# A layer with a bidirectional state-space mixer: output weights summed by DMA, fills of the scan divided anew, groups and regions in natural order

## Chip, core and metric

The kernel runs on one core of one Trainium2 chip. The metric is device time in microseconds, from the run's start to its end. A profiled execution has a second, slightly shorter figure, its span from the first to the last instruction; all places in the trace are microseconds from the start of that span. The engines are named as in the profile: PE (TensorE, with PEld its weight load), DVE (VectorE), ACT (ScalarE), POOL (GpSimd), SP (SyncE, which here only issues DMAs). "ACTq" or "SPq" is an instruction that the engine's sequencer does itself, such as issuing a DMA.

## What is computed

One layer over 1024 latent tokens of 1024 channels, with 256 context tokens ahead of them. All numbers are float32. Cut to what matters here:

```python
h_l = modulate(rms_norm(x, norm_mix), m_l[0], m_l[1])    # m_l, m_c: six rows each of silu(c) @ ada_w + ada_b
h_c = modulate(rms_norm(ctx, norm_mix), m_c[0], m_c[1])
# S5: 64 groups of 16 channels, 64 complex states each, two directions; the latent scan starts from the context's last state
lam_bar = exp(lam * exp(log_step)); b_bar = ((lam_bar - 1) / lam)[..., None] * b
h[t] = lam_bar * h[t-1] + b_bar @ u[t];   y[t] = real(c @ h[t])
y = y_fwd + y_bwd + d_skip * h_l
g = gelu(y)
x = x + m_l[2] * (g * sigmoid(g @ w_glu + b_glu))
h = modulate(rms_norm(x, norm_ffn), m_l[3], m_l[4])
x = x + m_l[5] * ((silu(h @ w1) * (h @ w3)) @ w2)
out = rms_norm(x, norm_final)
```

## The kernel before

**Chunks and quarters.** The tokens are cut into chunks of T = 8: 32 chunks of context and 128 of latents, 160 columns. The 64 groups are handled in four quarters q of 16, and for the products in eight blocks of 8. A chunk's contribution to the state comes from products (`sums`, in the loop over `hb`), and lands in `STQ[q]`, a view of the large region `ra`: 160 columns, real and imaginary part, 16 entries (a group pair of one direction each). `ra` is 80.5 KB per partition, 20.125 KB for each quarter; the first 4 KB of each quarter's part hold the context's columns, which are dead once the context's last state (column 31) is known.

**The scan** (`scan`, L790) runs on DVE over all quarters at once: 32 steps that advance two chunks, on the odd columns of the first half, then 63 steps of one chunk. A step is four dependent instructions. The even columns of the first half are filled in behind it from their neighbours ("fills": `fill_ops`, four instructions for four columns of half a quarter, on DVE, one or two dropped into each step by `one`; `fill`, L818, on POOL, four instructions for 16 columns of half a quarter). Before, DVE fills quarters 0, 2 and 3, POOL quarter 1.

**What runs beside the scan** is a list written by hand, the string that `run` (L909) walks through. The order within each engine's queue, and on each engine that issues DMAs, is the order of that string; engines wait for each other by semaphores. Its letters:

- A n: the adaLN gate rows, up to weight tile n of 64 (`ada`, L510): one product per tile of 256 KB, which SP loads eight tiles ahead into stages in the regions c2 and c1 (`stg`). M0, M1, M2 (`mod_cols`, L825): the finished rows are copied by ACT into `r8`, turned by PE, copied again, and finished on POOL.
- L q: load quarter q's C matrices into `Cs[q % 2]` (L634), a DMA issued by ACT; G q: sign them on ACT (`cs_sign`, L637).
- C q p: piece p of quarter q's output weights (`cl_gen`, L643): two POOL products of 128x1024, one into the weights `CL[q]` (region c q), one into an operand buffer `ct`; then their sum. Quarter 0 sums on PE (two products with the identity per half, and ACT copies the sum back), quarters 1 to 3 by a DMA that accumulates, issued by POOL (L658).
- K (`k_mats`, L757): the kernel matrices of half a quarter, out through two small staging buffers to DRAM by ACT's queue (L773); T u (`toeplitz`, L775): read back by SP as a banded matrix for the block half u, into four places `KQ`, which lie in the context columns of quarters 2 and 3. B q: move quarter q's input matrices for K into the place of the powers that C 0 and C 1 have used up.
- R k, P k, Y (L936 to L943): for block k, ACT copies the early states (columns 31 to 94) into `HSe` in eight instructions, PE multiplies inputs and early states into two PSUM tiles (of three), ACT copies them to `Y`, which lies over the inputs.
- F: a fill on POOL. Z i: the first two copies of late states (`late_restack`, L904), shared by ACT, DVE and POOL.

**Behind the list** a loop (L1039) takes the eight blocks in the order `order`: late products (`late_mm`), their sum into `Y`, GELU, the turned halves (`gt_hi`, `gt_lo`) into regions that the output weights leave free, and the first GLU products. Then come the GLU and the SwiGLU network, which hold PE from about 305 us to the end.

**Regions.** c0 to c3 are 16 KB each: the output weights of quarter q, and before and after them stages, operands and the GLU's tiles. `rxc` (8 KB) has both `Cs` places, later two `HSl` places and weights; its second half is also the operand buffer of C32 and C33, since `Cs[0]` is dead by then.

Of the kernel before, what the change touches and what calls it, by code (L numbers as in the profile page):

```python
# [11 lines left out]
R32 = mybir.dt.float32r  # L12
# [5 lines left out]
P = 128  # L18
# [5 lines left out]
T = 8  # L24
G = 64
HC = 16
# [11 lines left out]
def s5_ffn_kernel(tc, a, out):  # L38
    nc = tc.nc
    V, S, E, PE, SY = nc.vector, nc.scalar, nc.gpsimd, nc.tensor, nc.sync  # L40
    ctx = ExitStack()
    with ctx:
        ctx.enter_context(tc.manual_schedule())
        sb = ctx.enter_context(tc.tile_pool(name="sb", bufs=1))
        def region(tag, kb, dt=F32):
            return sb.tile([P, int(kb * 256)], dt, tag=tag, name=tag)

        def view(reg, kb, shape, parts=P):
            off = int(round(kb * 256))
            n = int(np.prod(shape))  # L50
            v = reg[:parts, off:off + n]
            if len(shape) > 1:
                names = "abcdef"[:len(shape)]
                v = v.rearrange(f"p ({' '.join(names)}) -> p {' '.join(names)}",
                                **{k: d for k, d in zip(names, shape)})
            return v

        R0 = region("r0", 7)
        RA = region("ra", 80.5)
# [51 lines left out]
        STB = 20.125  # L111
# [476 lines left out]
        def rot(*args):  # L588
            for op in rot_ops(*args):
                op()  # L590
# [46 lines left out]
        def cs_sign(q):  # L637
            S.activation(Cs[q % 2][:, 0], Cs[q % 2][:, 0], AF.Copy, scale=sgn[:, 1:2])
            S.activation(Cs[q % 2][:, 1], Cs[q % 2][:, 1], AF.Copy, scale=-1.0)
# [3 lines left out]
        def cl_gen(q, part, ct, how):  # L643
# [15 lines left out]
            else:  # L659
# [10 lines left out]
                 7: [(1, [0], 0, 8)], 8: [(1, [0], 8, 16)], 9: [(1, [1, 2, 3])],  # L670
                 11: [(2, [0], 0, 8)], 12: [(2, [0], 8, 16)], 13: [(2, [1, 2, 3])],
                 14: [(3, range(4), 0, 8)]}
        ct0 = [view(RC[1], i, [8, T, HC]) for i in (12, 4)]
        ct1 = [view(RC[3], i, [8, T, HC]) for i in (0, 4)]
        for hb in range(16):
            sums(hb)
            ada1(1, *ADA1.get(hb, ()))
# [63 lines left out]
        st1, st2 = (t[:, 384:512].rearrange("p (q r e) -> p q r e", r=2, q=4) for t in (LTb, ltc))  # L741
        sf = [LTa[:, 384:448], LTa[:, 448:512]]
        cs_load(1, S)
        cs_sign(1)
        kt = pA.tile([P, 2, 240], F32, tag="r3", name="kt")
        S.copy(kt.rearrange("p a b -> p (a b)"), cpk[:, 0:1].to_broadcast([P, 480]))

# [37 lines left out]
        def fill_ops(q, h, j):  # L785
            st = STQ[q][:, :, :, 8 * h:8 * h + 8]
            o = rot_ops(st[:, 32 + 8 * j:39 + 8 * j:2], st[:, 31 + 8 * j:38 + 8 * j:2], LQ[0], 16 * q + 8 * h, V, sf)
            return [o[0], o[2], o[1], o[3]]

        def scan():  # L790
            rest = []

            def one():
                if rest:
                    rest.pop(0)()

            def step(lq, i, o):
                products(st1, st2, STE[:, i], lq)
                tt(STE[:, o], st1, STE[:, o], ADD)
                one()  # L800
                tt(STE[:, o], st2, STE[:, o], ADD)
                one()

            for k in range(32):
                step(LQ[1], 31 + 2 * k, 33 + 2 * k)
                if k % 4 == 3:
                    for d in range(2):
                        rest.extend(fill_ops(0, d, k // 4))
            for q in (2, 3):
                for j in range(8):  # L810
                    for d in range(2):
                        rest.extend(fill_ops(q, d, j))
            for k in range(64, 127):
                step(LQ[0], 31 + k, 32 + k)
            while rest:
                one()

        def fill(q, h, reg, kb):  # L818

            tmps = [view(reg, kb + i, [256]) for i in range(2)]  # L820
            st, c0 = STQ[q], 32 * h
            for e in (0, 8):
                rot(st[:, 32 + c0:63 + c0:2, :, e:e + 8], st[:, 31 + c0:62 + c0:2, :, e:e + 8], LS[:, 0], 16 * q + e, E, tmps)

        def mod_cols(part):  # L825
            r8 = view(RC[2], 0, [4, P])
            if part == 0:
                S.copy(r8, pm.rearrange("p (j n) -> p j n", j=4))
            elif part == 1:
                pt = pw()  # L830
                for j in range(4):
                    PE.transpose(pt[:, j], r8[:, j], ident)
                for h in range(2):
                    S.copy(mcol[:, :, 4 * h:4 * h + 4].rearrange("p b j -> p j b"), pt[:, :, h:P:32])
            elif part == 2:
                tt(mcol, mcol, modb[:, 2:6], ADD, E)
                E.tensor_copy(mod2[:, 0], mcol[:, 1])
                tt(mod2[:, 1], mcol[:, 2], epsc[:, 1:2].to_broadcast([P, T]), ADD, E)
                tt(mod2[:, 1], mod2[:, 1], nrm[:, 1], MUL, E)
# [8 lines left out]
        def hstate(reg, kb):  # L848

            return view(reg, kb, [2, 2, 2, 64, 2])  # L850
# [42 lines left out]

        scan()
        inner, hse = {}, {}
        ct2 = [view(RC[3], i, [8, T, HC]) for i in (8, 12)]
        ct3 = [view(RXc, 4, [8, T, HC])]
        cts = [ct0 * 2, ct1 * 2, ct1 * 2, ct2 + ct3 * 2]

        HSl = [hstate(RXc, 0), hstate(RXc, 4), hstate(RA, STB), hstate(RA, 2 * STB)]  # L900
        HSe = [hstate(*((RC[3], 8 + 4 * (i % 2)) if i < 4 else (RA, STB * (i % 2)))) for i in range(8)]
        order = (6, 7, 4, 5, 0, 1, 2, 3)

        def late_restack(i):  # L904

# [3 lines left out]
        def run(prog):  # L909


            for w in prog.split():
                op, i = w[0], int(w[1:])
                if op == "A":
                    ada(i)
                elif op == "M":
                    mod_cols(i)
                elif op == "K":
                    k_mats(*divmod(i, 2))
                elif op == "Z":  # L920
                    late_restack(i)
                elif op == "L":
                    cs_load(i, S)
                elif op == "G":
                    cs_sign(i)
                elif op == "B":
                    j = 48 - HC * i
                    S.copy(BBc[:, :, :, j:j + HC], BB[:, :, HC * i:HC * i + HC].rearrange("p d g h -> p g d h"))
                elif op == "C":
                    q, part = divmod(i, 10)  # L930
                    cl_gen(q, part, cts[q][part], HOW[q][part])
                elif op == "F":
                    fill(*divmod(i, 10), *((RC[3], 4) if i < 20 else (RXc, 4)))
                elif op == "T":
                    toeplitz(i)
                elif op == "R":  # L936
                    hse[i] = HSe[i]
                    for d in range(2):
                        restack(hse[i], 4 * i, d, 0, (S, S, S, S))
                elif op == "P":  # L940
                    inner_mm(i, hse[i])
                elif op == "Y":
                    S.copy(yview(i), inner[i])  # L943

        HOW = ((PE,) * 4,) + ((SY,) * 4,) * 3
        run("A8 A12 C00 A20 C01 A26 C02 A32 C03 A38 K0 A42 K1 A46 L2 C10 A50 C11 A54 A58 A64 M0 M1 C12 T0 T1 T2 T3 C13 F10 F11 G2 B3 B2 K2 K3"
            " L3 C20 C21 M2 R0 P0 T4 T5 R1 P1 Y0 Y1 T6 T7 G3 C22 C23 R2 Y2 Y3 P2 R3 Y4 Y5 P3 Y6 Y7 K4 K5 T8 T9 T10 T11"
            " C30 C31 C32 C33 R4 P4 K6 K7 Y8 Y9 T12 T13 R5 P5 Y10 Y11 T14 T15 R6 P6 R7 Y12 Y13 Z1 Z0 P7 Y14 Y15")
        psW.__exit__(None, None, None)
        psA.__exit__(None, None, None)  # L950

# [87 lines left out]
        for i in range(10):  # L1039
            if i < 8:  # L1040
                ps_[i] = late_mm(i)
            if i + 2 < 8:
                late_restack(i + 2)
            if i == 3:
                HH = region("c3", 16, R32)
                GH[0] = (view(HH, 0, [4, 8, P]), view(region("c2", 16, R32), 0, [4, 8, P]))
            if i >= 3:
                pt = gt_hi(order[i - 3], 0, V if i in GHV else S)
            if 1 <= i < 9:
                late_add(i - 1, ps_[i - 1])  # L1050
            if i >= 3:
                gt_lo(order[i - 3], 0, pt)
            if 1 <= i < 9:
                late_act(i - 1)
            if i == WSP[0]:
                W0 = region("c0", 16, R32)
                WR.append((view(W0, 0, [8 * 256]), view(W0, 8, [8 * 256])))
            if i in WSP:
                j = 1 - WSP.index(i)
                v = slice(1024 * j, 1024 * j + 1024)  # L1060
                split(wr0[j], (WR[0][0][:, v], WR[0][1][:, v]), WSE[j], WSC[j])
            for s in PRE.get(i, ()):
                glu_mm(0, s, order[:5])
        X1 = region("c1", 16)
        xs = [view(X1, 4 * i, [D]) for i in range(4)]
        wraw = view(RXc, 0, [2048])

# [172 lines left out]

        w2raw = view(RU, 32, [D])
        tmp = [view(r, kb + 2 * i, [512]) for r, kb in ((RU, 36), (RXa, 0)) for i in range(2)]
        G2 = region("c1", 16, R32)
        GB = [[view(g, kb + 4 * i, [D]) for i in range(4)] for g, kb in ((G2, 0), (GR, 32))]

        def gb(ft):
# [324 lines left out]
```

## Time and profile before

| | |
|---|---|
| Time, median of 3 runs | 1082.42 us (1079.47 to 1082.84) |
| The profiled execution's own time | 1085.82 us |
| Its span | 1084.0 us, 16631 instructions |
| PE busy | 990.4 us, 91% of the span |
| PE's weight loads | 790.4 us, 73% |
| DVE busy | 762.3 us, 70% |
| POOL busy | 631.4 us, 58% |
| ACT busy | 418.7 us, 39% |
| DMA | 104.60 MB, 96 GB/s over the span |

The profile's busy shares are averages over stages with different limits. A row of the timeline gives the start, the length, the engine, the source line, the operation with what it writes and reads and its shape, how many in a row, and in brackets the idle time before and what ended it. Nearly all of DVE's and POOL's arithmetic goes through one helper, so it stands under L70, and is told apart by tiles: `c` is one of the regions c0 to c3, `ra` and `rxc` the regions above, `lta`, `ltb`, `ltc` tables in PSUM, `kd` the kernel matrices in DRAM.

### The profile page before, as it was taken

Reading aid. Unit: us, or ns where it says so; the run is one execution under the profiler, and the core shown is the slowest. Engines: PE = TensorE matmul, PEld = TensorE weight load, DVE = VectorE, ACT = ScalarE, POOL = GpSimd, SP = SyncE. Lnnn points to the kernel's source line nnn. Section 1 sums busy time; section 2 is a strip of 40 time slices with the busy share of each in tenths; the row PEclk is TensorE's granted clock in tenths of the full one; section 3 lists DMA queues with packets and bytes.
Section 4 is the critical chain, followed back from the end, with each engine's and each line's share of the span. In section 5 each row is a group of like instructions: output and inputs, shape, how many; then the busy total and the mean of one; then the engine's idle time right before and its main releaser. Section 6 shows DMA issues by size and latency. Waiting matters only on the chain.

```text
span 1084.0 us, 16631 instructions
## 1 busy us (share of the span) xinstructions
PE 990.4 (91%) x6088; PEld 790.4 (73%) x6088; DVE 762.3 (70%) x1783; ACT 418.7 (39%) x833; POOL 631.4 (58%) x501
## 2 busy tenths in 40 slices
PE   4898795656899999999999999999999999999997
PEld 1466521345799997887888888888888888888875
DVE  8979699970665686898766666666766666666657
ACT  4477620453964565423122222222222222222236
POOL 4599666881274364966565555665555555556563
PEclk9998997987999999999999999999999999999999
DMA  8966679675333102110111111111011111111104
GB/s 310 318 124 125 187 231 312 185 142 118 104 114 116 42 2 78 59 38 21 58 59 59 59 59 59 59 59 32 31 56 59 59 59 59 60 59 59 55 23 156
DMA packets 54946, 104.60 MB, mean 96 GB/s; under 512 B 4432, under 2 KB 25168, under 8 KB 53840
## 3 DMA queue, kind: packets, MB, share of 16 engines
q1 hardware_dynamic: 46656, 85.57, 23.7%
q0 software_dynamic: 3888, 14.16, 7.0%
q10 hardware_dynamic: 4320, 3.81, 1.1%
q8 instruction: 48, 0.79, 0.3%
q14 instruction: 34, 0.28, 0.1%
HBM read 83.20 MB, written 6.16 MB: 82 GB/s over the span
## 4 chain that ended last, share of the span: by engine, by line
PE 71%; DMA 9%; POOL 6%; DVE 6%; ACT 5%; issue 2%; SPq 1%; ACTq 0%; DVEq 0%; POOLq 0%
PE pu L1261 11%; PE pu L1260 11%; PE pu L1259 11%; PE pd L1259 7%; PE pd L1260 7%; PE pd L1261 7%; PE pe L1024 3%; PE pe L1025 3%; PE pe L1023 3%; DVE ru L70 2%; POOL c L70 2%; DMA c<-in_ada_w 2%; DMA kd<-r 1%; PE pm L514 1%; DVE rxa L70 1%
## 5 line engine op out<-in xcount | busy, mean ns | idle before, releaser
L70 POOL TENSOR_TENSOR c<-rxc,c 128x512 fp32r<-128x512 f32 x128 | 167.8, 1326 | 185.1 <-ACT c L1201 180.2
L70 DVE TENSOR_TENSOR ru<-pd,ru 128x512 f32<-128x512 f32 x336 | 226.5, 690 | 0.0
L1259 PE MATMUL pu<-ra,c 128*128 128x512 f32 x432 | 168.4, 390 | 0.6 <-ACT ra L1201 0.3
L1261 PE MATMUL pu<-ra,c 128*128 128x512 f32 x432 | 168.4, 390 | 0.6 <-POOL c L70 0.6
L1260 PE MATMUL pu<-ra,c 128*128 128x512 f32 x432 | 168.2, 389 | 0.6 <-DVE ra L70 0.6
L1201 ACT CAST c<-rxc 128x512 fp32r<-128x512 f32 x128 | 76.8, 617 | 188.0 <-POOL rxc L70 107.3
L1259 PE MATMUL pd<-c 128*128 128x512 f32 x336 | 131.0, 390 | 0.7 <-DVE ru L70 0.7
L1260 PE MATMUL pd<-c 128*128 128x512 f32 x336 | 130.7, 389 | 0.0
L1261 PE MATMUL pd<-c 128*128 128x512 f32 x336 | 130.7, 389 | 0.0
L70 DVE TENSOR_TENSOR ru<-pu,ru 128x512 f32<-128x512 f32 x84 | 57.8, 688 | 83.2 <-PE pu L1261 52.4
L70 POOL TENSOR_TENSOR c<-ru,c 128x1024 fp32r<-128x1024 f32 x22 | 53.0, 2407 | 81.7 <-ACT c L1002 73.0
L1261 PEld LDWEIGHTS pu<-ra,c 128*128 128x128 f32 x432 | 81.1, 188 | 18.5 <-POOL c L70 1.7
L1259 PEld LDWEIGHTS pu<-ra,c 128*128 128x128 f32 x432 | 81.1, 188 | 18.1 <-ACT ra L1201 0.8
L1260 PEld LDWEIGHTS pu<-ra,c 128*128 128x128 f32 x432 | 81.1, 188 | 17.7 <-POOL c L70 0.9
L1259 PE MATMUL pu<-c,c 128*128 128x512 f32 x192 | 74.9, 390 | 0.0
L1261 PE MATMUL pu<-c,c 128*128 128x512 f32 x192 | 74.7, 389 | 0.0
L1260 PE MATMUL pu<-c,c 128*128 128x512 f32 x192 | 74.7, 389 | 0.0
L1259 PEld LDWEIGHTS pd<-c 128*128 128x128 f32 x336 | 63.1, 188 | 15.0 <-DVE ru L70 1.9
L1261 PEld LDWEIGHTS pd<-c 128*128 128x128 f32 x336 | 63.1, 188 | 13.2
L1260 PEld LDWEIGHTS pd<-c 128*128 128x128 f32 x336 | 63.1, 188 | 12.9
L70 POOL TENSOR_TENSOR c<-rxc,rxa 128x1024 f32<-128x1024 f32 x30 | 62.0, 2138 | 16.2 <-PE pw L655 10.4
L70 DVE TENSOR_TENSOR ru<-ru,rxa 128x512 f32<-128x512 f32 (+1 forms) x62 | 62.5, 1008 | 7.1 <-ACT ru L1420 3.1
(333 smaller groups left out, 2137.3 us busy)
## 6 DMA issues: line engine op xcount, KB each, us to landing
c<-in_ada_w SPq DMA_DIRECT2D x64, 256.0 KB, 5.4
ru<-in_w SPq DMA_DIRECT2D x22, 512.0 KB, 3.6
c<-c POOLq DMA_DIRECT2D x20, 512.0 KB, 6.7
rxc<-in_w SPq DMA_DIRECT2D x38, 256.0 KB, 4.5
rxc<-in_w SPq DMA_DIRECT2D x19, 512.0 KB, 5.1
ra<-in_ada_w SPq DMA_DIRECT2D x10, 512.0 KB, 11.9
ru<-in_xT SPq DMA_DIRECT2D x4, 1024.0 KB, 8.5
ra<-kd SPq DMA_DIRECT2D x16, 256.0 KB
```

The costliest lines, as they stand in the source:

```text
L70: eng.tensor_tensor(out=o, in0=x, in1=y, op=op)
L514: PE.matmul(pm[32 * b:32 * b + 2], sc3[:, k, 1 - h:3 - h], ada_tile(i), start=i < 4, stop=i >= 60, tile_position=(0, 32 * b))
L1023: PE.matmul(pz, h_[:, k], wH[:, k], start=n == 0, stop=False)
L1024: PE.matmul(pz, h_[:, k], wL[:, k], start=False, stop=False)
L1025: PE.matmul(pz, l_[:, k], wH[:, k], start=False, stop=n == 7)
L1201: S.copy(o[0], x)
L1259: PE.matmul(pu, wh, bh, start=start, stop=False)
L1260: PE.matmul(pu, wh, bl, start=False, stop=False)
L1261: PE.matmul(pu, wl, bh, start=False, stop=stop)
```

## The change

- All sixteen pieces of output weights are summed by an accumulating DMA. The operand buffers are three: one in c1 and two in c3 (`c1`, `c3[0]`, `c3[1]`); quarter 3 keeps its two in c3's upper half and the one in `rxc`.
- Fills: DVE takes quarters 0 and 1 and the first half of quarter 2 in the scan; POOL takes the second half of quarter 2 and quarter 3 (F21, F30, F31), with temporaries in `rxc`, placed behind C33 in the list. `fill` now takes one half of the entries over all 32 columns.
- Early states `HSe` lie in the context columns of quarters 0 and 1 for all blocks; before, blocks 0 to 3 used c3's upper half. The fourth late place `HSl[3]` moves to the start of `ra`.
- The late products take the blocks 0 to 7 in order, the GLU's regions and weight halves follow (c0 and c1 for the turned halves, c2 for the weights, c3 for x).
- The list is rewritten: G1 is in it (before, the sign of quarter 1's C stood behind its load), pieces C 2 0 and C 2 1 stand directly behind M1, `r8` lies at the end of c2, K2, K3 stand behind R0 and R1, L3 behind K3, K4 and K5 before R2, Z0 and Z1 apart.

```diff
-        ct0 = [view(RC[1], i, [8, T, HC]) for i in (12, 4)]
-        ct1 = [view(RC[3], i, [8, T, HC]) for i in (0, 4)]
...
         cs_load(1, S)
-        cs_sign(1)
...
             for k in range(32):
                 step(LQ[1], 31 + 2 * k, 33 + 2 * k)
                 if k % 4 == 3:
-                    for d in range(2):
-                        rest.extend(fill_ops(0, d, k // 4))
-            for q in (2, 3):
+                    for h in range(2):
+                        rest.extend(fill_ops(0, h, k // 4))
+            for q, hs in ((1, (0, 1)), (2, (0,))):
                 for j in range(8):
-                    for d in range(2):
-                        rest.extend(fill_ops(q, d, j))
+                    for h in hs:
+                        rest.extend(fill_ops(q, h, j))
...
-        def fill(q, h, reg, kb):
-
-            tmps = [view(reg, kb + i, [256]) for i in range(2)]
-            st, c0 = STQ[q], 32 * h
-            for e in (0, 8):
-                rot(st[:, 32 + c0:63 + c0:2, :, e:e + 8], st[:, 31 + c0:62 + c0:2, :, e:e + 8], LS[:, 0], 16 * q + e, E, tmps)
+        def fill(q, h):
+
+            tmps = [view(RXc, 4 + i, [256]) for i in range(2)]
+            st = STQ[q][:, :, :, 8 * h:8 * h + 8]
+            for c0 in (0, 32):
+                rot(st[:, 32 + c0:63 + c0:2], st[:, 31 + c0:62 + c0:2], LS[:, 0], 16 * q + 8 * h, E, tmps)
 
         def mod_cols(part):
-            r8 = view(RC[2], 0, [4, P])
+            r8 = view(RC[2], 14, [4, P])
...
-        ct2 = [view(RC[3], i, [8, T, HC]) for i in (8, 12)]
-        ct3 = [view(RXc, 4, [8, T, HC])]
-        cts = [ct0 * 2, ct1 * 2, ct1 * 2, ct2 + ct3 * 2]
-
-        HSl = [hstate(RXc, 0), hstate(RXc, 4), hstate(RA, STB), hstate(RA, 2 * STB)]
-        HSe = [hstate(*((RC[3], 8 + 4 * (i % 2)) if i < 4 else (RA, STB * (i % 2)))) for i in range(8)]
-        order = (6, 7, 4, 5, 0, 1, 2, 3)
+        c3 = [view(RC[3], 4 * i, [8, T, HC]) for i in range(4)]
+        c1, cx = view(RC[1], 12, [8, T, HC]), view(RXc, 4, [8, T, HC])
+        cts = [[c3[1], c1, c3[0], c3[1]], [c1, c3[0], c3[1], c3[0]], [c3[0], c3[1]] * 2, [c3[2], c3[3], cx, cx]]
+
+        HSl = [hstate(RXc, 0), hstate(RXc, 4), hstate(RA, STB), hstate(RA, 0)]
+        HSe = [hstate(RA, STB * (i % 2)) for i in range(8)]
+        order = tuple(range(8))
...
-                    cl_gen(q, part, cts[q][part], HOW[q][part])
+                    cl_gen(q, part, cts[q][part], SY)
...
-        HOW = ((PE,) * 4,) + ((SY,) * 4,) * 3
-        run("A8 A12 C00 A20 C01 A26 C02 A32 C03 A38 K0 A42 K1 A46 L2 C10 A50 C11 A54 A58 A64 M0 M1 C12 T0 T1 T2 T3 C13 F10 F11 G2 B3 B2 K2 K3"
-            " L3 C20 C21 M2 R0 P0 T4 T5 R1 P1 Y0 Y1 T6 T7 G3 C22 C23 R2 Y2 Y3 P2 R3 Y4 Y5 P3 Y6 Y7 K4 K5 T8 T9 T10 T11"
-            " C30 C31 C32 C33 R4 P4 K6 K7 Y8 Y9 T12 T13 R5 P5 Y10 Y11 T14 T15 R6 P6 R7 Y12 Y13 Z1 Z0 P7 Y14 Y15")
+        run("A8 A12 C00 A16 C01 A20 A24 G1 C02 A28 C03 A32 C10 A36 A40 K0 A44 K1 L2 C11 A48 A52 C12 A56 G2 A60 T0 T1 T2 T3 C13 A64 M0"
+            " M1 C20 C21 R0 P0 R1 K2 Y0 Y1 P1 K3 B3 B2 L3 T4 T5 Y2 Y3 T6 T7 C22 C23 M2 G3 K4 K5 R2 P2 R3 Y4 Y5 P3 C30 C31 C32 C33 F21 F30 F31"
+            " Y6 Y7 T8 T9 T10 T11 R4 P4 K6 K7 Y8 Y9 T12 T13 R5 P5 Y10 Y11 T14 T15 R6 P6 Z0 Y12 Y13 R7 P7 Z1 Y14 Y15")
...
-                HH = region("c3", 16, R32)
-                GH[0] = (view(HH, 0, [4, 8, P]), view(region("c2", 16, R32), 0, [4, 8, P]))
+                HH = region("c0", 16, R32)
+                GH[0] = (view(HH, 0, [4, 8, P]), view(region("c1", 16, R32), 0, [4, 8, P]))
...
-                W0 = region("c0", 16, R32)
+                W0 = region("c2", 16, R32)
...
-                j = 1 - WSP.index(i)
+                j = WSP.index(i)
...
-        X1 = region("c1", 16)
+        X1 = region("c3", 16)
...
-        G2 = region("c1", 16, R32)
+        G2 = region("c3", 16, R32)
```

More of the change, by code (lines that the diff above doesn't have):

```diff
@@ L930, in run @@
                     q, part = divmod(i, 10)
-                    cl_gen(q, part, cts[q][part], HOW[q][part])
+                    cl_gen(q, part, cts[q][part], SY)
                 elif op == "F":
-                    fill(*divmod(i, 10), *((RC[3], 4) if i < 20 else (RXc, 4)))
+                    fill(*divmod(i, 10))
                 elif op == "T":
```

## The prediction, made before the changed kernel was built

> **What bounds the kernel now.** I read the busy time by stretch first (windows cut where the page's slices change), then the chain of waits between 125 and 310 us, then the timelines of ACT, POOL, PE and DVE there, and last the DMA part of the page. Columns of the stretch view: engine busy times, granted clock, share of the 16 DMA engines, GB/s.
>
> ```profile
> 131.00:160.00 29.00, 25.25 (x79) 6.63 (x72) 28.45 (x154) 5.03 (x9) 21.03 (x12) 0.94 0.70 230
> 160.00:190.00 30.00, 17.27 (x213) 5.53 (x213) 30.00 (x172) 2.61 (x6) 17.95 (x14) 0.78 1.03 305
> 238.00:280.00 42.00, 24.45 (x363) 20.96 (x365) 2.70 (x8) 21.17 (x51) 9.75 (x10) 0.80 0.52 119
> 280.00:305.00 25.00, 22.67 (x315) 20.71 (x311) 21.94 (x42) 20.28 (x36) 9.54 (x14) 1.00 0.43 157
> 305.00:1084.00 779.00, 768.60 (x3794) 651.00 (x3792) 527.64 (x846) 263.52 (x515) 439.80 (x310) 1.00 0.17 57
> ```
>
> From 305 us on TensorE is busy 768.6 of 779 us and the change touches nothing in it but region names; so what the change wins or loses before that passes to the end whole. Between 280 and 305 us (late products, GELU, first transposes) DVE has 21.9 of 25 us; the order of groups and the regions are renamed there, with the same instructions. The change lives between 131 and 280 us. Three of its sub-stretches differ: the weights of the adaLN gates saturate the DMA engines from 160 to 190 us (share 1.03); a chain of copies follows; from 238 to 280 us no engine is full, so waits set the end.
>
> ```profile
> 131.37 10.19 DMA rxc<-in_cxy
> 167.64 7.25 DMA kd<-r
> 178.22 8.46 DMA c<-in_ada_w
> 203.66 3.73 DMA kd<-r
> 240.44 4.95 DMA c<-rxc
> 247.77 8.22 DMA c<-rxc
> 276.50 1.16 PE pw L886 x8
> 277.66 1.90 PE pw L891 x32
> 279.56 4.52 PE pe L968 x80
> ```
>
> These links of the chain (start, length) say what to follow: the gate weights until 198 us, then ACT's copies, then the sums of quarter 3's output weights, C32 and C33 (`c<-rxc`), whose second landing (256.0) lets K6 start, and 23.6 us later P7's products end (279.56) and the late products begin. I call T the start of M0, ACT's copy of the finished gate rows; now T = 198.38, and P7 ends at T + 81.2.
>
> **DMA: four more sums.** C00 to C03 change from eight pairs of TensorE products and eight ACT copies to four accumulating DMAs of 512 KB.
>
> ```profile
> q0 software_dynamic: 3888, 14.16, 7.0%
> c<-c POOLq DMA_DIRECT2D x20, 512.0 KB, 6.7
> c<-rxc POOLq DMA_DIRECT2D x7, 512.0 KB, 5.0
>   DMA c<-in_ada_w: 39.6, 31
> ```
>
> q0 carries exactly the 27 sums: 7.0% of 1084 us is 75.9 us of all 16 engines, 2.8 us a sum. Four more cost 11.2 us of DMA time before the gate stream ends, and the gate products wait for that stream (39.6 us in 31 waits, last row). Idle DMA time that can take them: 30% of 29 us between 131 and 160 us, 8.7 us. From 160 to 190 us there is none. So the stream, and T, come (11.2 - 8.7) / 1.03 = 2.4 us later. The other way works TensorE: it no longer sits in front of C00 to C03's products, so the ring of eight stages is refilled sooner. I take **T + 2**, bounds -2 (all in idle time, and the ring gains) and +8.2: only C00's DMA ends before the loads resume at 141.6, the other three displace weights, 8.4 / 1.03.
>
> The Trainium skill, "DMA: Bandwidth & Descriptors", section on the anatomy of a DMA on the gpsimd path, fits 2.0 us plus bytes over 436 GB/s; by it 512 KB move in an estimated 1.2 us, four in 4.8, and T would not move. The 2.8 us of q0 speak against it, and the sum goes by them.
>
> POOL's own work: today TensorE's share of a piece holds POOL's next one up (5.91 us idle, first row below). In the new form a piece takes two products and an issue, 167.60 to 172.80 = 5.2 us. With three operand buffers, a buffer comes back two or three pieces later, 10 us, beyond the landing of 6.7; eight pieces from 131 us on end near 173 to 177, and C13 ends at 177.1 today. TensorE's removed pieces cost nothing to lose: it waits for weights.
>
> ```profile
> 151.08 5.99 POOL L70 TENSOR_TENSOR c<-rxc,rxa 128x1024 f32<-128x1024 f32 x3 [5.91 <-PE pw L655]
> 167.60 4.29 POOL L70 TENSOR_TENSOR c<-rxc,rxa 128x1024 f32<-128x1024 f32 x2
> 172.80 4.29 POOL L70 TENSOR_TENSOR c<-rxc,rxa 128x1024 f32<-128x1024 f32 x2
> 225.56 3.99 POOL L70 TENSOR_TENSOR c<-rxc,rxa 128x1024 f32<-128x1024 f32 x2 [3.20 <-ACT c L868]
> 245.46 2.01 POOL L70 TENSOR_TENSOR rxc<-rxc,rxa 128x1024 f32<-128x1024 f32 x1 [2.10 <-DMA c<-rxc]
> L70 POOL TENSOR_TENSOR ra<-ra,c 128x256 f32<-128x256 f32 x8 | 5.8, 721 | 0.3
> L70 POOL TENSOR_TENSOR c<-ra,r 128x256 f32<-128x256 f32 x8 | 5.6, 719 | 8.4 <-DVE ra L70 8.4
> ```
>
> **ACT's order from M0 to G3.** ACT sets the pace after T.
>
> ```profile
> 198.38 0.58 ACT L828 COPY c<-pm 128x512 f32<-128x512 f32 x1 [21.43 <-PE pm L514]
> 200.99 1.14 ACT L928 COPY rxa<-c 128x512 f32<-128x512 f32 x2
> 202.01 0.37 ACT L772 COPY r<-kt 128x240 f32<-128x240 f32 x1
> 203.28 0.36 ACT L772 COPY r<-kt 128x240 f32<-128x240 f32 x1 [0.90 <-PE kt L771]
> 208.23 0.65 ACTq L635 DMA_DIRECT2D rxc<-in_cxy  x1
> 208.92 7.02 ACT L868 COPY c<-ra 64x256 f32<-64x256 f32 x16 [1.09 <-DVE ra L70]
> 215.96 1.07 ACT L943 COPY ru<-pw 128x512 f32<-128x512 f32 x2
> 217.06 0.72 ACT L638 ACTIVATE rxc<-rxc,r 128x512 f32<-128x512 f32 x1
> ```
>
> Now L3 (the load of quarter 3's C) is issued at T + 9.9, ahead of R0 and R1 (16 copies, 7.0 us), which cover its flight: G3 at 217.06 waits for nothing. In the new order R0, R1, K2, Y0, Y1, P1's products, K3 and B3, B2 all stand ahead of L3, and only Y2, Y3 between L3 and G3. Step by step: M0, M1 to T + 1.6; R0, R1 7.0, to 8.6; K2's two copies (1.27 apart) 2.0, to 10.6; Y0, Y1 1.1, to 11.7; P1 needs the PSUM that Y0 frees and ends 3 us later (1.2 + 1.9 as P7's halves), to 14.4; K3's copies to 17.1; B3, B2 1.1, to 18.2. G2 is gone from this stretch (1.1 us, hidden in the gate stream). L3 so starts 8.3 us later. **Its flight is now in the open**: bounds 3.7 us (the small `kd` write in a quiet moment) and 10.2 (the load at 131 us, among weights); around T + 20 only C23's sum and four small reads run, so I take 6: G3 starts at T + 24.2 and C30 half a microsecond behind it, T + 24.9. Before, C30 started at 225.56, T + 27.2, held by R3's copies through the early states' place in C's region (3.20 <- ACT); the places in `ra` remove that hold.
>
> C20 and C21 no longer wait for r8 (moved to the end of its region) nor for the fills F10, F11 (11.4 us of POOL, moved to DVE): they need G2 and the gate tiles 56 to 59, which are read before the last four, so before T. Started even at T, four pieces of 5.2 us and a landing of 6.7 bring C23 home at T + 27.5, 2 us behind the first use (K4 behind G3, T + 25.4) and well before C33's place; started 5 us earlier, as I take it, it is covered.
>
> **C30 to C33, K6, fills.** From C30's start to C33's issue now 247.77 - 225.56 = 22.2 us; the same operand buffers, the same waits (2.10 for C32's landing). C33's landing takes 8.2 where C32's took 5.0, because the four reads for T8 to T11 lie on top of it:
>
> ```profile
> 242.26 5.00 SPq L781 DMA_DIRECT2D ra<-kd  x4
> 232.69 0.36 ACT L772 COPY r<-kt 128x240 f32<-128x240 f32 x1
> 238.48 0.33 ACTq L773 DMA_DIRECT2D kd<-r  x1
> 256.85 0.36 ACT L772 COPY r<-kt 128x240 f32<-128x240 f32 x1 [14.63 <-PE kt L771]
> 261.63 0.33 ACTq L773 DMA_DIRECT2D kd<-r  x1
> ```
>
> In the new order K4, K5 take T + 25.4 to 31.2 (5.8 us); R2, R3 (7.0) and Y4, Y5 (1.1) bring ACT to T + 39.3, R4 follows P3 and Y6, Y7 near T + 44; the four reads, free once K5's write has landed (31.2 + 3.7), are issued between T + 35 and 43. C33 is issued at T + 24.9 + 22.2 = 47.1, alone: 5.0, landing at **T + 52.1** (T + 57.6 before).
>
> Behind it: 0.8 to the first copy (255.99 to 256.85), K6, K7 5.1, Y8, Y9 1.1, R5 3.5 (half of 7.02), P5's last products and one copy 2.4 (1.9 + 0.5), R6 3.5, P6's last products 1.9 with Z0's three copies under them, Y12, Y13 1.1, R7 3.5, P7's last products 1.9: 24.8 us against 23.6, the difference being Z0 and Y12, Y13 ahead of R7. The moved fills stand on POOL behind C33's landing, whose operand place they use: 24 instructions at 0.72 us, 17.3 us; F21 ends 5.8 us behind the landing where R5 starts at 7.0, F30 11.5 against 12.9, F31 17.3 against 19.4. **Margins of one to two microseconds**; if ACT got there sooner, the fills would be next.
>
> P7 ends at T + 52.1 + 24.8 = T + 76.9 instead of T + 81.2: 4.3 us sooner.
>
> **No cost, with cover:** DVE's scan loses 32 of 192 fill instructions; they sit in gaps between dependent steps, and only the ten behind the last step shorten it, 2.6 us. What follows on DVE is
>
> ```profile
> 256.21 1.35 DVE L870 COPY rxc<-ra 64x256 f32<-64x256 f32 x3 [19.53 <-DMA c<-rxc]
> ```
>
> after 19.5 idle us, so nothing waits for it; R4 would, if it came before the scan's end near 234 us; it comes at T + 44. Quarter 1's fills end two thirds through the scan, long before R2. G1 behind A24 finds its load landed; `kt`'s clearing loses its wait. Late restacks, GLU regions and weight halves in natural order keep counts and distances of reuse: 0, bounds -1 to +1.
>
> **Sum:** +2.0 - 4.3 = **-2.3 us**, for the profiled execution a span of 1081.7 instead of 1084.0; it ran 1085.8 with what lies around it, 3.4 above the median of 1082.42. Against that median: **1080.1**.
>
> **Rivals.** (a) *The gate stream pays in full*: T moves by 8.2 instead of 2, and -4.3 + 8.2 = +3.9: 1086.3. For it: share 1.03 for 30 us, and L2, now behind a later K0, holds the last weights' slots. Against it: the idle 8.7 us. It turns the result slower from T = 198.4 + 4.3 = 202.7 on. The Trainium skill's page on DMA, section on SWDGE, HWDGE and iDMA, says each engine takes its software and hardware queues in turn, which would make each sum displace weights at once; the 8.46 us of a weight load in the busy stretch, against 2.91 in a quiet one, fit that.
>
> ```profile
> 141.63 2.91 DMA c<-in_ada_w
> ```
>
> (b) *The stream is not late*, since TensorE's holds were as costly as the sums: T unchanged, -4.3, 1078.1; with T two earlier 1076.1. For it: POOL and TensorE hold each other up today (5.91 us). Against it: the 27 sums at 2.8 us. (c) *The wait for L3 takes the place of the one removed*: flight 10.2 as at 131 us puts C30 at T + 29.1, and all behind it 4.2 later: -2.3 + 4.2 = +1.9, 1084.3; with C33's landing again under reads (8.2 for 5.0) +5.1, 1087.5. Against it: fewer bytes in flight there.
>
> **Chances.** Forecast 0.42 (own range 1077.5 to 1083), (a) 0.22, (b) 0.25, (c) 0.11. A difference of 0.3%, 3.2 us, is about what can be told from no change. Of the forecast 0.15 lies beyond it and 0.27 within; (b) is faster; of (a) 0.19 is slower, of (c) 0.07, the rest within: faster 0.40, same 0.34, slower 0.26. The range goes a little past (b)'s better end and to (c)'s worse: 1074.5 to 1087.5.
>
> **What would show it.** M0's copy at 199 to 202 us; G3 on ACT behind an idle of 4 us or so ended by the load of C; C30 within a microsecond of G3; C33's landing in about 5 us, near 252; POOL's 24 fills ending before R7; P7's last products near 277. The prediction is wrong if M0 comes after 202.7, if any of R5 to R7 waits for POOL, or if R1's or R0's copies wait for the scan.

## The result and the profile after

The changed kernel takes 1113.09 us, median of 4 runs (1110.74 to 1114.68), against 1082.63 (1079.47 to 1084.36, 4 runs) before: a ratio of 1.0283, 95% interval 1.0252 to 1.0314. It is slower by some 30 us where 2.3 us less were forecast. The profiled execution has a span of 1110.4 us (1084.0 before).

ACT's timeline of the changed kernel from T on, with the last row of DVE's scan behind it (start, length, what, and in brackets the idle time before and what ended it; the code's lines are three lower than before, so the restack's copy is L865):

```profile
195.75 0.59 ACT L825 COPY c<-pm 128x512 f32<-128x512 f32 x1 [7.39 <-PE pm L514]
197.22 3.43 ACT L865 COPY ra<-ra 64x256 f32<-64x256 f32 x8
230.83 3.31 ACT L865 COPY ra<-ra 64x256 f32<-64x256 f32 x8 [30.18 <-DVE ra L70]
247.49 0.72 ACT L638 ACTIVATE rxc<-rxc,r 128x512 f32<-128x512 f32 x1 [1.59 <-DMA rxc<-in_cxy]
255.76 6.90 ACT L865 COPY ra<-ra 64x256 f32<-64x256 f32 x16 [0.40 <-ACT r L769]
...
230.50 0.29 DVE L70 TENSOR_TENSOR ra<-ltc,ra 128x128 f32<-128x128 f32 x1
```

R0's eight copies run at T + 1.5. R1's eight do not follow: ACT stands still for 30.18 us until DVE's scan is over at 230.79, and everything queued behind R1 on ACT waits with it: K2 and K3's copies, L3, G3. POOL's queue shows what that does to quarter 3's sums:

```profile
248.29 3.99 POOL L70 TENSOR_TENSOR c<-rxc,rxa 128x1024 f32<-128x1024 f32 x2 [34.96 <-ACT rxc L638]
...
271.89 2.01 POOL L70 TENSOR_TENSOR rxc<-rxc,rxa 128x1024 f32<-128x1024 f32 x1 [5.97 <-DMA c<-rxc]
```

C30 starts at T + 52.5, where the prediction had T + 24.9. The stretch view of the same 39 us, of the kernel before and then of the changed one (busy time of PE, PEld, DVE, ACT, POOL; granted clock; DMA share; GB/s):

```profile
199.00:238.00 39.00, 24.45 (x516) 21.20 (x516) 37.33 (x210) 23.72 (x55) 32.20 (x23) 0.96 0.69 149
```

```profile
199.00:238.00 39.00, 6.72 (x124) 5.83 (x124) 31.07 (x161) 6.62 (x16) 13.29 (x12) 0.61 0.30 62
331.50:1110.40 778.90, 768.41 (x3792) 650.80 (x3790) 528.67 (x846) 263.50 (x515) 440.59 (x310) 1.00 0.17 57
```

In the changed kernel's first row only DVE still has its work; PE and ACT have lost nearly three quarters of theirs, POOL more than half. The second row answers to the 779 us from 305 us on in the prediction: PE has 768.41 us there against 768.60. So the whole difference of the spans, 26.4 us, arises ahead of the late products: from T to P7's end it takes 29.0 us more, and T itself stands 2.6 us earlier in this profile (195.75 against 198.38). The chain of waits from 150 to 310 us gives the members:

```profile
by line: DVE ra L70 16.1%; DMA c<-in_ada_w 13.7%; DMA c<-rxc 8.4%; ACT ra L865 7.7%; DVE ltb L70 6.9%; POOL c L70 6.3%; DVE ltc L70 6.0%; PE pw L888 5.3%; DMA kd<-r 4.7%; issue 3.5%; DVE lta L70 3.3%; POOL rxc L70 2.5%; DMA rxc<-in_cxy 2.3%
...
230.83 0.41 ACT ra L865
243.84 3.63 DMA rxc<-in_cxy
248.29 4.00 POOL c L70 x2
262.98 8.84 DMA c<-rxc
274.20 4.56 DMA c<-rxc
304.34 1.58 PE pw L888 x24
```

DVE's scan leads it: no row of the prediction's chain was DVE's. P7's products end at 305.9 (last row) against 279.6, 26.3 us later. C32's landing, 8.84 us where the prediction had about 5, is the second thing that it did not have.

### The profile page after: what moved, and what is told of

It is laid out like the page before. It is cut to its first block, busy times and chain, and to the rows that moved or that the text cites. A ratio compares the mean times of both kernels' runs of the same rounds, so it can differ in the third digit from the quotient of the medians.

```text
span 1110.4 us, 16539 instructions
## 1 busy us (share of the span) xinstructions
PE 994.9 (90%) x6056; PEld 789.9 (71%) x6056; DVE 761.1 (69%) x1751; ACT 414.2 (37%) x825; POOL 641.8 (58%) x513
## 4 chain that ended last, share of the span: by engine, by line
PE 67%; DVE 13%; DMA 7%; POOL 6%; ACT 4%; issue 2%; ACTq 0%; DVEq 0%; POOLq 0%
PE pu L1257 11%; PE pu L1256 11%; PE pu L1255 11%; PE pd L1255 7%; PE pd L1257 7%; PE pd L1256 7%; DMA c<-in_ada_w 3%; DVE ra L70 3%; PE pe L1020 3%; PE pe L1021 3%; POOL c L70 3%; PE pe L1019 3%; DVE ru L70 2%; DMA c<-rxc 1%; DVE rxa L70 1%
## 5 line engine op out<-in xcount | busy, mean ns | idle before, releaser
L1197 ACT CAST c<-rxc 128x512 fp32r<-128x512 f32 x128 | 76.9, 617 | 190.1 <-POOL rxc L70 107.5
L1257 PEld LDWEIGHTS pu<-ra,c 128*128 128x128 f32 x432 | 81.1, 188 | 18.5 <-POOL c L70 1.7
L1255 PEld LDWEIGHTS pd<-c 128*128 128x128 f32 x336 | 63.1, 188 | 14.9 <-DVE ru L70 1.9
```

The lines of the kernel that those rows point to most:

```text
L1197: S.copy(o[0], x)
L1255: PE.matmul(pu, wh, bh, start=start, stop=False)
L1257: PE.matmul(pu, wl, bh, start=False, stop=stop)
```

## Experiments

Times are medians; the ratio is to runs of the kernel before on the same chip, with its 95% interval. The letter and digit ahead of a kernel's name stand for it in the text.

| kernel | what it is | us (range, runs) | ratio |
| --- | --- | --- | --- |
| e1_r1_place | changed, R1's place outside `ra` | 1082.7 (1080.3 to 1086.3, 12) | 1.0005 (0.9985 to 1.0024) |
| e2_before_r1_place | before, R1's place as changed | 1104.29 (1103.1 to 1105.2, 5) | 1.0209 (1.0176 to 1.0242) |
| e3_r1_low | changed, R1 in R0's place | 1084.93 (1079.6 to 1086.2, 12) | 1.0015 (0.9996 to 1.0033) |
| i1_flat_view | changed, ACT's destination written flat | 1082.6 (1077.9 to 1084.1, 12) | 0.9998 (0.9979 to 1.0018) |
| f1_two_places | changed, other places for R0 and R1 | 1083.25 (1079.4 to 1085.7, 12) | 0.9988 (0.9969 to 1.0007) |
| e5_before_dma_sums | before, quarter 0 summed by DMA | 1084.64 (1081.9 to 1092.1, 12) | 1.0030 (1.0007 to 1.0054) |
| g1_q0_by_tensore | f2, quarter 0 summed by TensorE | 1077.9 (1076.3 to 1079.8, 10) | 0.9951 (0.9935 to 0.9967) |
| f2_c33_own_operand | f1, C33 with its own operand place | 1079.99 (1076.4 to 1084.2, 12) | 0.9971 (0.9954 to 0.9988) |
| f3_k2_k3_l3_early | f1, K2, K3, L3 ahead of M0 | 1087.41 (1085.2 to 1090.0, 12) | 1.0036 (1.0017 to 1.0054) |
| g2_order_and_places | g1, new order from M1 to G3 | 1076.44 (1069.2 to 1079.2, 8) | 0.9934 (0.9905 to 0.9964) |
| i2_best_k6_early | g2, flat, K6 ahead of R4 | 1078.4 (1075.1 to 1081.9, 12) | 0.9962 (0.9944 to 0.9980) |
| b1_before_again | before, once more | 1079.42 (one run, span 1077.6) | |

### R1's wait: the place, the source, or the way the place is written

The theory after the first trace: R1 waits because its early state now lies in quarter 1's context columns, between columns that the scan still updates. The rivals: its source (the fills were divided anew), or the loss comes from the order and the DMA sums and the wait only shows it.

R1's place alone taken out of the change:

```diff
-        HSe = [hstate(RA, STB * (i % 2)) for i in range(8)]
+        HSe = [hstate(*((RC[3], 12) if i == 1 else (RA, STB * (i % 2)))) for i in range(8)]
```

> The changed kernel with R1's early state alone put into the last 4 KB of quarter 3's weights; all else as changed. Main theory (R1's new place in quarter 1's context columns makes it wait for the scan): R1 follows R0 without a wait near 201 us, L3, G3, C30 and P7's end all come about 30 us earlier (C30 near 218, P7's end near 276), 1080 to 1085 us. Rival one (R1 waits for its source, through the new division of the fills): R1 still waits 30 us, 1110 to 1115. Rival two (the order from M0 to G3, or the four more DMA sums, take the time): R1's wait goes but at most 10 us come back, above 1100.

1082.7 us. R1 follows R0 at once (201.09 in the row below); P7 ends at 276.2. The new place holds the second direction's B until K2, K3, B3 and B2 have read it, so these work on other numbers here and the output is not the layer's; the instructions are the same.

```profile
197.63 3.44 ACT L865 COPY ra<-ra 64x256 f32<-64x256 f32 x8
201.09 3.44 ACT L865 COPY c<-ra 64x256 f32<-64x256 f32 x8
```

The other way round, R1's place alone put into the kernel before:

```diff
-        HSe = [hstate(*((RC[3], 8 + 4 * (i % 2)) if i < 4 else (RA, STB * (i % 2)))) for i in range(8)]
+        HSe = [hstate(*((RC[3], 8 + 4 * (i % 2)) if i in (0, 2, 3) else (RA, STB * (i % 2)))) for i in range(8)]
```

> The kernel before with one edit: R1's early state in quarter 1's context columns, as in the change; the fills, the sums and the order stay. Main theory: R1, which started at 212.4 us, waits for the scan's end near 236.7, 24 us, and everything behind it on ACT moves by that: 1102 to 1108 us. Rivals one and two: no new wait, 1081 to 1085.

1104.29 us, and the wait appears with before's fills, sums and order:

```profile
201.91 3.44 ACT L868 COPY c<-ra 64x256 f32<-64x256 f32 x8 [1.48 <-DVE ra L70]
230.29 3.32 ACT L868 COPY ra<-ra 64x256 f32<-64x256 f32 x8 [24.93 <-DVE ra L70]
...
229.97 0.28 DVE L70 TENSOR_TENSOR ra<-ltc,ra 128x128 f32<-128x128 f32 x1
232.75 0.22 DVE L70 TENSOR_TENSOR ra<-ra,lta 128x64 f32<-128x64 f32 x1
```

Both rivals fall: written as it is, the copy waits in this place and not in the other, whatever else was changed. In the kernel before it costs 2.09%, 22.6 us of the 24.93. The last two rows say what it waits for: the scan's last step, which writes one column of all four quarters and ends at 230.25. The fills behind it, which write quarter 3 alone and end at 232.97, do not hold it.

Is it any place in `ra`? R1 in R0's own place, the first 4 KB, below every column that the scan touches:

```diff
-        HSe = [hstate(RA, STB * (i % 2)) for i in range(8)]
+        HSe = [hstate(RA, STB * (i % 2) * (i > 1)) for i in range(8)]
```

> The changed kernel with R1's early state in quarter 0's context columns, in the same region and in R0's own place, which lies below every column that the scan still touches. Main theory: no wait for the scan, but one for P0's products, which read that place: R1 starts 1.5 to 3 us later than with a place of its own outside the region, 1081 to 1088. If any place in this region made a restack wait for the scan: 1110 to 1115, and rival one says the same.

1084.93 us, and no wait for the scan. R1 starts 1.46 us behind R0's end. The row names no releaser; P0's products, which read that place, run on PE from 199.56 to about 202, so the short wait is put down to them:

```profile
196.81 3.50 ACT L865 COPY ra<-ra 64x256 f32<-64x256 f32 x8
201.77 3.46 ACT L865 COPY ra<-ra 64x256 f32<-64x256 f32 x8 [1.46 <-issue]
```

Yet R1's bytes and the scan's are different bytes: the scan updates columns 31 and up of each quarter, the early state fills the columns below. The last test of this group leaves every place as changed and writes the same 256 numbers of the destination as one run instead of a 2 x 64 x 2 view:

```diff
-                        S.copy(dst, src)
+                        S.copy(dst.rearrange("p a j e -> p (a j e)"), src)
```

> The changed kernel with every place, every instruction and the order as changed; only the destination of ACT's restack copies is written as one run of 256 numbers instead of a 2 x 64 x 2 view of the same 256. If the wait for the scan comes from the bytes that R1 shares or nearly shares with the scan, or from its source, it stays: 1110 to 1115 us. If it comes from the way the destination is described to whatever puts in the waits (a place between the scan's columns, given in runs of two, is taken for an overlap): R1 follows R0, R3 no longer waits for the scan's end either, 1079 to 1084 us.

1082.6 us, no different from before:

```profile
197.52 6.86 ACT L865 COPY ra<-ra 64x256 f32<-64x256 f32 x16
227.03 6.98 ACT L865 COPY ra<-ra 64x256 f32<-64x256 f32 x16 [0.40 <-DVE ra L70]
...
230.71 0.29 DVE L70 TENSOR_TENSOR ra<-ltc,ra 128x128 f32<-128x128 f32 x1
```

R0 and R1 are one stretch of 16 copies, and R3, in the same place as R1, follows R2 at about 230.5, half a microsecond ahead of the end of the scan's last row (231.00). So the 30 us were no dependence of the data: one line, which leaves every byte where it was, removes them. The reading that fits is that the waits are put in when the kernel is built, from the way each instruction's reads and writes are written down, and that a place between the scan's strided columns, given in runs of two numbers, was taken for an overlap with the scan. That step itself was not looked into, and which other shapes are taken so was not tried.

A version with two places that need neither, R0 in the end of quarter 2's weights and R1 in quarter 0's context columns, serves as base for what follows:

```diff
-        HSe = [hstate(RA, STB * (i % 2)) for i in range(8)]
+        HSe = [hstate(*((RC[2], 12) if i == 0 else (RA, STB * (i % 2) * (i > 1)))) for i in range(8)]
```

> The changed kernel with the early states of R0 in quarter 2's last 4 KB of weights (free until C23) and of R1 in quarter 0's context columns; all else as changed. Main theory: neither restack waits for the scan nor for P0's products; R1 ends near T + 8.5, P7 near T + 80, 1080 to 1085 us, within 0.3% of the kernel before. If the rest of the change also cost tens of us: above 1090.

1083.25 us, as expected.

### The four sums by DMA

With R1 mended, the change still gains nothing. Its first term was T + 2 for four more sums by DMA. The sums by DMA alone, in the kernel before, with three operand buffers in turn for quarters 0 and 1:

```diff
-        cts = [ct0 * 2, ct1 * 2, ct1 * 2, ct2 + ct3 * 2]
+        t0, t1, t2 = ct1[1], ct0[0], ct1[0]
+        cts = [[t0, t1, t2, t0], [t1, t2, t0, t2], ct1 * 2, ct2 + ct3 * 2]
...
-        HOW = ((PE,) * 4,) + ((SY,) * 4,) * 3
+        HOW = ((SY,) * 4,) * 4
```

> The kernel before with C00 to C03 summed by DMA and three operand buffers for quarters 0 and 1, as in the change; places, fills and order stay. By the prediction's term T comes 2 us later (bounds -2 to +8.2): 1084.4, from 1080 to 1091. By the changed kernel's trace, where T stands 67.5 us behind C00's start against 67.1: no more than +1, 1082 to 1084.

1084.64 us, 1.0030 (1.0007 to 1.0054), that is 3.2 us (0.8 to 5.8): the prediction's term of 2 lies inside, and the median is above what the changed kernel's trace beside the first profile had suggested. To see how much T varies by itself, the kernel before once more:

> The kernel before, profiled once more, to see how far its time from C00's start to T (67.1 us in the first profile) and C00's start itself (131.3) vary: the traces of the other kernels, whose code is the same up to C00, have C00 at 127.6 to 128.4. Expected: C00 near 128, T - C00 between 64 and 67, P7's end at T + 81, span 1079 to 1081.

1079.42 us, T 62.9 us behind C00, P7's end at T + 80.6. The first profile of before was of a late execution (1085.82 us against a median of 1082.42), this one is of an early one: C00, ahead of which no code differs, started at 131.30 there and at 129.16 here, and from C00's start to T it took 67.1 us there and 62.9 here. All profiles but one (f3, below, whose order puts more ahead of T):

| sums of quarter 0 | T minus C00's start, us |
|---|---|
| TensorE: first profile, b1, e2, g1, g2, i2 | 67.1, 62.9, 63.9, 62.7, 62.9, 62.4 |
| DMA: changed, e1, e3, e5, f1, f2, i1 | 67.5, 67.8, 67.7, 68.7, 71.4, 66.9, 67.7 |

The medians are 62.9 and 67.7: by the profiles the four sums put T 4.8 us later, more than the 3.2 us by which e5's time moved. The list's order up to T is not the same in all of these kernels; it is in the first profile, b1, e2 and e5. The stretch view from 131 to 160 us, b1 first, then e5, says where the time goes; behind each stands the accumulating queue's row:

```profile
131.00:160.00 29.00, 25.98 (x82) 7.13 (x80) 28.66 (x156) 6.20 (x11) 21.04 (x13) 1.00 0.83 254
...
q0 software_dynamic: 3888, 14.16, 7.1%
```

```profile
131.00:160.00 29.00, 19.22 (x38) 1.56 (x36) 28.73 (x158) 1.70 (x3) 27.22 (x18) 0.88 1.02 277
...
q0 software_dynamic: 4464, 16.25, 8.0%
```

q0 takes 8.0% of 1080.8 us against 7.1% of 1077.6, 10.0 us more for four sums. The DMA engines stood idle for 17% of the 29 us in b1, 4.9 us, not for the 30% of the first profile, which is the odd one: in the other five with TensorE's sums the share is 0.82 to 0.84. 10.0 less 4.9 are 5.1 us, close to the 4.8.

Quarter 0 summed by TensorE again in the mended change, from the kernel with C33's own operand (below):

```diff
-                    cl_gen(q, part, cts[q][part], SY)
+                    cl_gen(q, part, cts[q][part], PE if q == 0 else SY)
...
-        run("A8 A12 C00 A16 C01 A20 A24 G1 C02 A28 C03 A32 C10 A36 A40 K0 A44 K1 L2 C11 A48 A52 C12 ...
+        run("A8 A12 C00 A20 G1 C01 A26 C02 A32 C03 A38 K0 A42 K1 A46 L2 C10 A50 C11 A54 C12 ...
```

> The kernel with C33's own operand, with C00 to C03 summed by TensorE again and the gate tiles between the pieces spaced as before. T stood 66.9 to 71.4 us behind C00's start in the five traces with all sums by DMA, and 62.9, 63.9 and 67.1 in the three with TensorE's. If the four sums are the cause: T - C00 back at 63 to 65, 3 to 4 us off the time of the kernel with C33's own operand, 1075 to 1077 us. If the gate stream varies by itself from run to run: no change, 1079 to 1081.

1077.9 us. T minus C00's start is back at 62.7, 4.1 us less than the 66.9 of the kernel it came from, but the ratio fell from 0.9971 to 0.9951 only, 2.2 us, and the two intervals overlap. A part of the difference is seen: R3, in quarter 1's columns and written as in the change, now waited 3.61 us for the scan's end, which T does not move (0.75 us in f2):

```profile
230.46 3.34 ACT L865 COPY ra<-ra 64x256 f32<-64x256 f32 x8 [3.61 <-DVE ra L70]
```

### What is left of the gain from T to P7

The prediction had P7's end at T + 76.9; with the wait gone it is at T + 80.2 (i1), T + 79.0 (f1). In i1, POOL and SP around C32:

```profile
219.00 3.99 POOL L70 TENSOR_TENSOR c<-rxc,rxa 128x1024 f32<-128x1024 f32 x2 [6.20 <-ACT rxc L638]
...
233.69 0.88 POOL L658 DMA_DIRECT2D c<-rxc  x1 [0.30 <-POOL rxc L70]
234.30 2.32 POOL L70 TENSOR_TENSOR c<-rxc,rxa 128x1024 f32<-128x1024 f32 x1
242.54 2.02 POOL L70 TENSOR_TENSOR rxc<-rxc,rxa 128x1024 f32<-128x1024 f32 x1 [5.92 <-DMA c<-rxc]
244.86 0.88 POOL L658 DMA_DIRECT2D c<-rxc  x1 [0.30 <-POOL rxc L70]
249.56 1.40 POOL L70 TENSOR_TENSOR rxc<-ra,r 128x256 f32<-128x256 f32 x2 [3.82 <-DMA c<-rxc]
```

```profile
230.59 5.84 SPq L778 DMA_DIRECT2D ra<-kd  x4
```

The four reads for T8 to T11 are issued from T + 34.5 to T + 40.4, and C32's sum at T + 37.6 lies in the middle of them. C33's second product wants the buffer that C32's sum still reads, and POOL is idle for 5.92 us. C33 with an operand place of its own:

```diff
-        cts = [..., [c3[2], c3[3], cx, cx]]
+        cts = [..., [c3[2], c3[3], cx, view(RA, STB, [8, T, HC])]]
```

> The same with C33's second product in quarter 1's context columns instead of the buffer that it shares with C32. With R1's place mended the traces show POOL idle for 6 us before C33 (242.86 against 236.8), until C32's landing, which the four reads for T8 to T11 lengthen to 9 us. If that wait is what kept the predicted 4.3 us from coming (my sum had 2.1 us there): C33 is issued 4 to 6 us earlier, P7 ends near T + 75, 1076 to 1080 us. If ACT or the landing itself sets the pace: no change, 1080 to 1085.

1079.99 us, 0.9971 (0.9954 to 0.9988), from 0.9988 without it: P7 ends at T + 77.9. The direction is right, the gain at the low end, since the product now waits for P3 to leave that place (2.17 us); the intervals of the two overlap.

The order from M0 to G3, first by moving K2, K3, B3, B2 and L3 ahead of M0 and G3 behind M1 (from f1_two_places):

```diff
-        run("... C12 A56 G2 A60 T0 T1 T2 T3 C13 A64 M0"
-            " M1 C20 C21 R0 P0 R1 K2 Y0 Y1 P1 K3 B3 B2 L3 T4 T5 Y2 Y3 T6 T7 C22 C23 M2 G3 K4 K5 ...
+        run("... C12 C13 A56 G2 K2 A60 T0 T1 T2 T3 K3 B3 B2 L3 A64 M0"
+            " M1 C20 C21 G3 R0 P0 R1 Y0 Y1 P1 T4 T5 Y2 Y3 T6 T7 C22 C23 M2 K4 K5 ...
```

> The first kernel of this group with C13, K2, K3, B3, B2 and L3 put among the last gate tiles, ahead of M0, and G3 right behind M1: L3's flight no longer stands in the open, and C30 needs only C23 (POOL) ahead of it. If the order from M0 to G3 is what binds after T (C30 at T + 23 now): C30 near T + 17, C33's landing near T + 43, then ACT from the scan's end on sets the pace, P7 near T + 68 to 70; T itself may come 1 to 3 us later since the load and the small writes join the gate stream: 1069 to 1076 us. If C30's start does not matter: 1080 to 1086.

A miss: 1087.41 us. T came 74.2 us behind C00's start: the last gate products stood on PE behind K3's, which waited for ACT's copies (first two rows), and M0 stood on ACT behind the issue of the load, 2.43 us. Then G3, now ahead of R0, held ACT for the load's landing:

```profile
198.53 0.57 PE L760 MATMUL kt<-c,c 128*16 128x112 f32 x8 [4.19 <-ACT r L769]
199.46 1.93 PE L514 MATMUL pm<-c,r 128*2 128x512 f32 x8
...
200.55 2.43 ACTq L635 DMA_DIRECT2D rxc<-in_cxy  x1
...
203.08 0.59 ACT L825 COPY c<-pm 128x512 f32<-128x512 f32 x1 [1.44 <-issue]
...
213.01 0.72 ACT L638 ACTIVATE rxc<-rxc,r 128x512 f32<-128x512 f32 x1 [8.34 <-DMA rxc<-in_cxy]
```

Then after M1, from the kernel with TensorE's sums: K2 ahead of R0, K3 and L3 ahead of R1, G3 behind Y1, and R3 in quarter 0's columns too, as R4 already was, which frees C33's operand place:

```diff
-        HSe = [hstate(*((RC[2], 12) if i == 0 else (RA, STB * (i % 2) * (i > 1)))) for i in range(8)]
+        HSe = [hstate(*((RC[2], 12) if i == 0 else (RA, STB * (i % 2) * (i > 3)))) for i in range(8)]
...
-            " M1 C20 C21 R0 P0 R1 K2 Y0 Y1 P1 K3 B3 B2 L3 T4 T5 Y2 Y3 T6 T7 C22 C23 M2 G3 K4 K5 ...
+            " M1 C20 C21 K2 R0 P0 K3 B3 B2 L3 R1 Y0 Y1 G3 P1 T4 T5 Y2 Y3 T6 T7 C22 C23 M2 K4 K5 ...
```

> The same, with K2 ahead of R0, K3 and L3 ahead of R1 (R1, Y0 and Y1 cover L3's flight) and G3 behind Y1; R3's and R4's early states in quarter 0's context columns too, so that C33's operand in quarter 1's columns waits for nothing. If C30's start (T + 23 now, 3 us of it L3's flight) is what binds: C30 near T + 18, C33's landing near T + 44 instead of T + 52, P7 near T + 72, 1069 to 1074 us. If R2, which waits for DVE's fills, binds instead: a gain of 0 to 2 us over the kernel with TensorE's sums.

1076.44 us, 0.9934 (0.9905 to 0.9964): better than the kernel before and the changed one; against the version with TensorE's sums (0.9935 to 0.9967) the intervals overlap.

```profile
210.30 4.00 POOL L70 TENSOR_TENSOR c<-rxc,rxa 128x1024 f32<-128x1024 f32 x2 [2.59 <-ACT rxc L638]
...
227.98 2.32 POOL L70 TENSOR_TENSOR ra<-rxc,rxa 128x1024 f32<-128x1024 f32 x1
230.59 0.88 POOL L658 DMA_DIRECT2D c<-ra  x1 [0.30 <-POOL ra L70]
...
c<-ra POOLq DMA_DIRECT2D x1, 512.0 KB, 8.6
```

C30 stands at T + 18.5 as expected, and C33 is issued 230.59 - 191.79 = 38.8 us behind T; but its landing takes 8.6 us, for the four reads now lie over it, and comes at T + 47.4, not T + 44. P7 ends at T + 77.7 (80.6 without the new order), not T + 72: a third of the expected 8.6 us. The second row also writes the very place of the changed kernel's R1, 3 us ahead of the scan's last row in that trace (231.24), as 8 x 8 x 16 numbers, and does not wait: the place as such is not guarded.

Last, K6 ahead of R4 there, and the flat view:

```diff
-            " Y6 Y7 T8 T9 T10 T11 R4 P4 K6 K7 Y8 Y9 ...
+            " Y6 Y7 K6 T8 T9 T10 T11 R4 P4 K7 Y8 Y9 ...
```

> The kernel with the new order and places, with the flat destinations, and K6 ahead of R4 instead of behind P4. There C33 had landed near 234 us but K6's copies stood at 244, behind R4 and P4's products. If ACT's order binds there: K6's copies near 239, P7 3 to 4 us earlier, 1071 to 1074 us. If P4 or the writes to DRAM behind K6 bind: no change, 1075 to 1077.

No gain, 1078.4 us. The expectation took C32's landing near 234 for C33's, which comes at 231.3 + 8.5 = 239.8 here: K6's copies could not start before 240.7, R4 behind them moved from 238.1 in g2 to 242.7, and Y8 stood at 250.7 against 250.4. On ACT the two only changed places.

## Why the prediction was wrong

**The step that failed** is the early states' new places, priced as a pure gain ("the places in `ra` remove that hold", no wait among the terms). The text did name the event under what would make it wrong ("if R1's or R0's copies wait for the scan"), but no rival carried its price; all three rivals were about the gate stream and L3. The runs show a wait of 30.18 us at that place: the place alone makes it in the kernel before (24.93), and the destination's view alone takes it away (0.9998 instead of 1.0283). It needed no knowledge of the cause to price: R1 wrote into the region that DVE was updating, the scan's end stood near 234 us in the prediction's own text and R1 at T + 5.1 by its sum, about 204 to 206 us, so a wait for the scan had an upper bound of some 30 us, and that is what came.

**DMA: four more sums**, T + 2: inside its bounds (-2 to +8.2), but too small by the profiles, 4.8, halfway to rival (a); e5's time, 3.2 us (0.8 to 5.8), does not exclude 2. The price per sum held (2.5 us of 16 engines for 2.8); the idle DMA time was read from one late execution. The Trainium skill, "DMA: Bandwidth & Descriptors", section on the anatomy of a DMA on the gpsimd path, gives a fit by whose second term 512 KB move in an estimated 1.2 us; q0's 10.0 us for four speak against it here.

**ACT's order**, G3 at T + 24.2 and C30 at T + 24.9: in i1 218.20 and 219.00, T + 22.1 and T + 22.9. L3's flight did stand in the open: 5.2 us from its issue at 212.97 for the 6 priced, 2.87 of them idle.

**C30 to C33**, 22.2 us from C30's start to C33's issue: 25.9 (219.00 to 244.86). The reads were placed rightly, between T + 35 and 43, and laid over C33's old flight only; they fell on C32's. The prediction's own numbers had it: 14.9 us from C30 to C32 before (225.56 to 240.44) put C32 at T + 39.8. C33's landing, 5.0: 4.7.

**The tail** from landing to P7's end, 24.8: 26.7 in i1 (249.56 to 276.29). Of the excess 1.4 us is K6 and K7, whose copies came 1.63 us apart rather than 1.3 and waited 1.86 for a write to DRAM. The moved fills ended before R7 needed them: hidden, as predicted.

The four terms together: -2.0 + 3.7 - 0.3 + 1.9 = +3.3, which is 80.2 against 76.9. With T 2.8 later than priced, that is 6.1 us, more than the predicted gain of 2.3 even without R1's wait. It is also more than the times show: the sum would make i1 3.8 us slower than before, and it measured 0.9998 (0.9979 to 1.0018), 1.9 us slower at most. With e5's 3.2 us for the sums it would be 2.2. So the gain is gone, but how much of it each term took stays open to some 2 us.

**No cost**: right. The scan ended 102.6 us behind C00's start instead of 105.4 (e2), 2.8 us for the 2.6 predicted, and i1, without R1's wait, was no faster for it; the renamed late groups and GLU regions kept PE's 768 us.

## What to carry to other kernels

When a buffer moves into a region that another engine is still writing, price a wait for that engine's last instruction there first, whether or not the bytes meet; look at the first instruction that writes the new place and at what stands behind it in its queue. If the trace then shows a wait that the data do not need, try the same place written as a plain run before giving it up. And take idle time that is to absorb new work from more than one execution: with 0.83 of DMA share in place of 0.70, the prediction's own sum, (11.2 - 4.9) / 1.03, gives an estimated 6 us in place of 2; 3.2 to 4.8 were measured.

## What had not been expected of the hardware

The same instructions ahead of any changed code brought C00 at 127.6 to 131.3 us in fourteen profiles. The load of 512 KB of C took 3.63 us from issue to landing where the DMA share was 0.63 with the load itself in it (changed kernel, 243.84), and 12.4 beside three accumulating sums and the reads of `kd`, at a share of 1.02 (f3, 200.55 to 213.0).
